# Gates multiplied into the activation, down results in two float32r parts, and the fallback block moved to expert 25

## The chip, the cores and the metric

The program runs on one core of a Trainium2 chip. The metric is the device time of one execution in microseconds, the median of three timed executions. The engines are TensorE (PE, which runs matrix products and, beside them, loads of the stationary operand, PEld), VectorE (DVE), ScalarE (ACT), GpSimd (POOL) and SyncE (SP, which issues most DMAs). In rows the suffix q (PEq, SPq) means the sequencer of the engine. Tokens are 256, in two halves of 128 called tt.

## The reference

One layer: a token mixer (two kinds of attention), a layer norm, a mixture of experts with four of 32 experts for each token, and a second layer norm. The change touches the experts alone:

```python
logits = xt @ w_router + b_router
top_val, top_idx = lax.top_k(logits, 4)
gates = softmax(top_val)
...
h = xblk @ w_up[e] + b_up[e]
gate = min(h[..., ::2], 7.0)
up = clip(h[..., 1::2], -7.0, 7.0)
act = (up + 1.0) * (gate * sigmoid(1.702 * gate))
yblk = act @ w_down[e] + b_down[e]
...
y = zeros.at[token].add(yblk * gate_of_token)
```

Everything is float32. `w_up[e]` is 1024 x 2048 (8 MB), `w_down[e]` 1024 x 1024 (4 MB), so 384 MB of expert weights are read once.

## The kernel before, in words

The mixer fills the first 241 us of the execution; it is the same in both kernels. Then one unrolled Python loop goes over the 32 experts. An expert has S = 64 slots. Tokens get into slots by one-hot products, not by indexed transfers, as follows.

- **Place and gather** (L696, L709). DVE compares a token's rank within the expert (`rankp`) with an iota and makes a bf16 one-hot `ph` (tokens x slots). 48 bf16 products (L714; 8 blocks of columns, 2 halves of tokens, 3 bf16 parts `hs` of the float32 activations) give `xg`, the 64 tokens of the expert, exact. The gather of expert e+1 runs inside expert e.
- **Up** (L731). A bias product (L741) starts each of two PSUM tiles h0 and h1; then 64 float32 products (L745) with the weights u0 and u1, 4 MB each. Each tile takes its half of the hidden columns.
- **SwiGLU** (L748) on DVE and ACT, into act0 and act1; **transposes** of both (L762, PSUM tile pt) and copies to actT (L763).
- **Down** (L765). 32 float32 products with the 4 MB d into PSUM (pd), copied to one of the two 64-row halves of `yb` (L928), which holds a pair of experts: an even one and the odd one behind it.
- **Way back** (L703, L720, L793). POOL makes `pg`, the one-hot of the pair times the gate, in float32; in the odd expert PE transposes it (L723) into `pgt`. In the next even expert `combine` adds the pair into the result `y` by four products that PE runs as float32 (eight rows of the trace, L796, 512 columns each). `y` stays in PSUM from the mixer to the end.

Each product of the combine and of the ups and downs is float32. `add_b_down` (L684) adds the down bias of all experts by the matrix of gates `gmat`; it is called in expert 22.

**Blocks that are rarely taken.** Tokens beyond 64 of an expert are handled by a first block at L896, behind the swiglu, and a second at L932, behind the down products. Each stands inside an If on a bit of a register; when it is not taken, every engine jumps over its code. In this input they are taken for experts 1 and 8. More than 128 tokens would need `general()` (L828), a loop over all experts whose code is emitted once, behind the last expert, inside an If at L969 that also holds a second copy of the final norm; it isn't taken here.

**Weights.** Five slots of 4 MB form a ring. Load k brings piece k of the order u0, u1, d of expert 0, 1, ... SP issues load(3e+5) and load(3e+6) behind the block at L896, and load(3e+7) at the end of expert e, behind the block at L932. Each load waits for PE to have read its slot.

**The order on PE** is the order of the code: bias, ups, (jump at L896), add_b_down in expert 22, combine in even experts, gather of the next expert, transposes, down, (jump at L932). There is no planner and no priority; what is written first goes first on each engine. At the end the last expert's down is cut in two halves (L777) with the combine of the first half in between, and `second_norm` (L946) writes the output.

Of the kernel before, what the change touches and what calls it, by code (L numbers as in the profile page):

```python
# [31 lines left out]
def tile_hybrid(ctx, tc, x, w_in, w_o, lambda_qk, subln_g, sinks, ln_g, ln_b,  # L32
                w_router, b_router, w_up, b_up, w_down, b_down, out):
    nc = tc.nc
# [36 lines left out]
    sel = keep.tile([96, NE], BF, name="sel")  # L71

# [343 lines left out]
    for k in range(3):  # L416
        nc.gpsimd.tensor_copy(sel[32 * k:32 * k + 32, :], ident[32 * k:32 * k + 32, 32 * k:32 * k + 32])
    for k in range(4):
        nc.gpsimd.tensor_copy(fold[32 * k:32 * k + 32, :], ident[32 * k:32 * k + 32, 32 * k:32 * k + 32])
# [230 lines left out]
    def gates():  # L650
        gate = mp.tile([128, 2, 4], F32, name="gate")
        gs = mp.tile([128, 2], F32, name="gs")
        eq = mp.tile([128, 2, 4, NE], F32, name="eq", tag="sg")
# [9 lines left out]
        nc.vector.tensor_reduce(gmat, eq.rearrange("p t k e -> p t e k"), AX.X, OP.add)  # L663

    def counts():
        cnt = mp.tile([1, 3, NE], F32, name="cnt", tag="sg")
# [17 lines left out]
    def add_b_down(bd):  # L684
# [3 lines left out]
        gT = mp.tile([NE, 2, 128], F32, name="gT", tag="sg")  # L688
# [14 lines left out]
    def place_back(pg, e, rk, r, n):  # L703

        for tt in range(2):
            nc.gpsimd.tensor_scalar(pg[:, tt], iota_s[:, None, :n].to_broadcast([128, r, n]), rk[:, tt:tt + 1],  # L706
                                    gmat[:, tt, e:e + 1], op0=OP.is_equal, op1=OP.mult)
# [11 lines left out]

    def way_back(pg, pgt=None, p=None):  # L720
# [3 lines left out]
        pgt = mp.tile([128, 2, 128], F32, name="pgt", tag="pgt") if pgt is None else pgt  # L724
# [23 lines left out]
    def swiglu(h, act, tmp=None):  # L748
        gt = h[:, :, :, 0].rearrange("p i c -> p c i")
        ut = h[:, :, :, 1].rearrange("p i c -> p c i")  # L750
        g, sg, u = tmp or (mp.tile([128, 2, 128], F32, name="g", bufs=1), mp.tile([128, 2, 128], F32, name="sg"),
# [5 lines left out]
        nc.vector.tensor_mul(act, u, sg)  # L757
# [7 lines left out]
    def down(d, n, actT, p=None):  # L765
# [4 lines left out]
        for k in range(8):  # L770
            q, c = divmod(k, 8 // G)
            for o in range(G):
                nc.tensor.matmul(p[o * n:(o + 1) * n, :w], actT[c // 2][:, c % 2, q * n:(q + 1) * n], d[:, k, o * w:(o + 1) * w],  # L773
                                 start=(k == 0), stop=(k == 7), tile_position=(0, o * n))
        return p

    def last_down(d, actT, yb):  # L777

        for ch in range(2):
            p = [pm.tile([128, 512], F32, name="pd", tag="m"), pm.tile([128, 512], F32, name="pd", tag=f"h{ch}", bufs=1)]  # L780
            for k in range(8):
                q, c = divmod(k, 4)
                for o in range(2):
                    cs = slice(ch * 512 + o * 256, ch * 512 + (o + 1) * 256)
                    nc.tensor.matmul(p[o][o * S:(o + 1) * S, :256], actT[c // 2][:, c % 2, q * S:(q + 1) * S], d[:, k, cs],
                                     start=(k == 0), stop=(k == 7), tile_position=(0, o * S))
# [35 lines left out]
    bd = mp.tile([NE, D], F32, name="bd", bufs=1)  # L822
    nc.sync.dma_start(out=bd, in_=b_down[0])
    xg_of, pgt, yb, pg = {}, None, None, None
    xg_of[0] = gather(place(rankp[:, :, 0], S), S)
    counts()
    gates()
    def general():  # L828

        d = ring[2]  # L830
# [4 lines left out]
        pgt2 = mp.tile([128, 2, 128], F32, name="pgt2", tag="pgt")  # L835
        pg2 = mp.tile([128, 2, 4, Q], F32, name="pg2", tag="pg")
# [3 lines left out]
        tmp = [mp.tile([128, 2, 128], F32, name=k, **kw) for k, kw in (("g", {"bufs": 1}), ("sg", {}), ("u", {"bufs": 1}))]  # L840
        m = [pm.tile([128, 512], F32, name=f"m{k}", tag="m") for k in range(2)]
        three = [m[k].rearrange("p (a b) -> p a b", b=128)[:, 0:2] for k in range(2)]
        for e in range(NE):
            def again(i):
                nc.sync.dma_start(out=df, in_=_rows(w_up, 128, e * D * 2048 + i * 8192, 16384, 8192))
                return d.rearrange("p (j a) c -> p j (a c)", a=2)

            with is_over(e, 1 if e else 0):
# [3 lines left out]
                with tc.For_i(1 if e else 0, n, 1):  # L852
                    nc.vector.tensor_scalar(rk, rk, float(Q), None, op0=OP.subtract)
                    place_back(pg2, e, rk, 4, Q)
                    place(rk, Q, ph2)
                    gather(ph2, Q, m[0].rearrange("p (a b) -> p a b", b=Q)[:, 0:8], xg2)
                    h2 = m[1].rearrange("p (i a b) -> p i a b", a=2, b=2)
                    for i in range(2):
                        up(e, Q, 0, h2, xg2, again(i), range(4 * i, 4 * i + 4))
                    swiglu(h2, act2, tmp)  # L860
                    nc.sync.dma_start(out=df, in_=_rows(w_down, 128, e * D * D, 8192, 8192))
                    more_down(d, act2, actT2, pg2, pgt2, yb2, three + [m[0]])
                    more_back(pgt2, yb2)

    for e in range(NE):
# [17 lines left out]
        if par == 1:  # L883
            pgt = way_back(pg)
        if e < NE - 2:
            for b in range(2):
                up(e, S, b, h[b], xg_of[e], u1, range(4, 8))
                swiglu(h[b], act[b])
        else:
# [3 lines left out]
            for b in range(2):  # L893
                swiglu(h[b], act[b])
        if e > 0:
            with is_over(e):  # L896
                act2 = mp.tile([128, 2, 128], F32, name="more", bufs=1)
                pg2 = mp.tile([128, 2, 4, Q], F32, name="pg2", tag="pg")
                rk = mp.tile([128, 2], F32, name="rk")
                nc.vector.tensor_scalar(rk, rankp[:, :, e], float(S), None, op0=OP.subtract)  # L900
                xg2 = gather(place(rk, Q), Q, pm.tile([128, 8, Q], F32, name="p", tag="h0", bufs=1))
                place_back(pg2, e, rk, 4, Q)
                h2 = h_tile(1)
                for i, u in enumerate((u0, u1)):
                    up(e, Q, 0, h2, xg2, u, range(4 * i, 4 * i + 4))
                swiglu(h2, act2)
# [7 lines left out]
        if e == 22:  # L914
# [7 lines left out]
        if par == 0:  # L922
            yb = mp.tile([128, 2, 512], F32, name="yb", bufs=1)
# [73 lines left out]
```

## Time and profile before

| | |
|---|---|
| timed executions | 1233.15, 1227.6, 1233.84 us (median 1233.15) |
| profiled execution, own time | 1228.62 us |
| its span in the profile | 1226.8 us |
| PE busy | 1105.1 us (90%) |
| DVE, ACT, POOL busy | 327.7, 200.8, 139.1 us |
| PEld (loads of stationary operands) busy | 514.3 us |
| DMA | 441.77 MB, mean 360 GB/s |

The page gives the busy time of each engine and 40 slices of the span, each about 30.7 us long. A digit is the busy share in tenths. In rows of a timeline the columns are the start in us from the start of the span, the length in us, the engine, the line of the kernel, the operation, the output and inputs, the tile's rows and columns, the type, and a count of joined instructions; in brackets stands the idle time of the engine before it and what ended that. "issue" in a bracket is time in which the engine waited for nothing that the profile shows. A line of the waits gives total idle time, how many times, and the longest.

### The profile page before, as it was taken

Reading aid. Unit: us, or ns where it says so; the run is one execution under the profiler, and the core shown is the slowest. Engines: PE = TensorE matmul, PEld = TensorE weight load, DVE = VectorE, ACT = ScalarE, POOL = GpSimd, SP = SyncE. Lnnn points to the kernel's source line nnn. Section 1 sums busy time; section 2 is a strip of 40 time slices with the busy share of each in tenths; the row PEclk is TensorE's granted clock in tenths of the full one; section 3 lists DMA queues with packets and bytes.
Section 4 is the critical chain, followed back from the end, with each engine's and each line's share of the span. In section 5 each row is a group of like instructions: output and inputs, shape, how many; then the busy total and the mean of one; then the engine's idle time right before and its main releaser. Section 6 shows DMA issues by size and latency. Waiting matters only on the chain. (4 is left out here: it accounts for less than half of the span.)

```text
span 1226.8 us, 17445 instructions
## 1 busy us (share of the span) xinstructions
PE 1105.1 (90%) x6841; PEld 514.3 (42%) x6841; DVE 327.7 (27%) x705; ACT 200.8 (16%) x425; POOL 139.1 (11%) x163
## 2 busy tenths in 40 slices
PE   7999999798989999989997999799998899979993
PEld 7989676333333333333332333233433233323332
DVE  4555964612111211221211111111121111111113
ACT  3765661401000000010000000000000000000000
POOL 1056562201000000000000000000000000000001
PEclk9999999899999999999998999899998899989998
DMA  9932528696799999969999999999999999999971
GB/s 327 360 131 119 206 82 330 248 418 271 292 426 423 420 426 426 427 276 427 427 426 425 426 426 426 427 426 426 425 425 426 402 408 422 425 427 418 420 298 39
DMA packets 46605, 441.77 MB, mean 360 GB/s; under 512 B 5120, under 2 KB 8320, under 8 KB 20512
## 3 DMA queue, kind: packets, MB, share of 16 engines
q1 hardware_dynamic: 46320, 439.52, 86.5%
q8 instruction: 101, 1.65, 0.5%
q14 instruction: 40, 0.33, 0.1%
q10 hardware_dynamic: 144, 0.26, 0.1%
HBM read 438.72 MB, written 1.05 MB: 358 GB/s over the span
## 5 line engine op out<-in xcount | busy, mean ns | idle before, releaser
L745 PE MATMUL h<-w,xg 128*64 128x512 f32 (+1 forms) x2176 | 470.2, 596 | 0.2 <-ACT xg L717 0.2
L745 PEld LDWEIGHTS h<-w,xg 128*64 128x64 f32 (+1 forms) x2176 | 150.2, 136 | 276.8 <-issue 265.4
L773 PE MATMUL pd<-w,actT 128*64 128x512 f32 x992 | 230.5, 616 | 0.3 <-issue 0.3
L773 PEld LDWEIGHTS pd<-w,actT 128*64 128x64 f32 x992 | 70.6, 142 | 138.9 <-issue 138.6
L706 POOL TENSOR_SCALAR pg<-iota_s,rankp,gmat 128x64 f32<-128x64 f32 x64 | 36.4, 581 | 792.9 <-PE p L723 773.5
L753 DVE TENSOR_SCALAR g<-h 128x256 f32<-128x256 f32 x66 | 28.0, 425 | 288.8 <-issue 159.1
L754 ACT ACTIVATE sg<-g 128x256 f32<-128x256 f32 x66 | 27.5, 417 | 468.9 <-DVE g L753 468.9
L714 PE MATMUL p<-ph,hs 128*128 128x64 bf16 (+1 forms) x1632 | 57.7, 197 | 37.5 <-issue 22.6
L161 POOL TENSOR_TENSOR lo<-w,hi 128x1024 fp32r<-128x1024 f32 x31 | 78.8, 2551 | 104.9 <-ACT hi L160 104.7
L928 DVE COPY yb<-pd 64x512 f32<-64x512 f32 x31 | 21.2, 684 | 247.3 <-PE pd L773 247.3
L714 PEld LDWEIGHTS <-hs 128*128 128x128 bf16 x1632 | 54.8, 101 | 62.0 <-issue 34.2
L796 PE MATMUL y<-yb,pgt 128*128 128x512 f32 x128 | 62.1, 628 | 8.4 <-DVE g L753 6.6
L928 ACT COPY yb<-pd 64x512 f32<-64x512 f32 x31 | 18.0, 582 | 238.9 <-DVE yb L928 135.7
L160 ACT CAST hi<-w 128x1024 fp32r<-128x1024 f32 x48 | 50.1, 1044 | 20.6 <-PE pj L199 13.8
L763 ACT COPY actT<-pt 128x256 f32<-128x256 f32 x64 | 23.9, 373 | 157.5 <-PE pt L762 157.2
L717 DVE COPY xg<-p 128x512 f32<-128x512 f32 x31 | 21.4, 691 | 100.7 <-PE p L714 100.7
L762 PE MATMUL pt<-ident,act 128*128 128x128 f32 x128 | 29.5, 316 | 19.2 <-ACT actT L763 16.8
L796 PEld LDWEIGHTS y<-yb,pgt 128*128 128x128 f32 x128 | 23.9, 197 | 47.1 <-issue 25.3
L188 PE MATMUL pj<-xh,hi 128*128 128x256 f32 x272 | 41.0, 295 | 2.3 <-ACT hi L160 1.6
L741 PE MATMUL h<-bups,sel 96*64 96x512 bf16 (+1 forms) x136 | 27.6, 420 | 16.0 <-PEq L932 16.0
L725 DVE COPY pgt<-p 128x256 f32<-128x256 f32 x18 | 7.6, 425 | 117.4 <-PE p L723 117.4
L188 PE MATMUL pj<-xl,hi 128*128 128x256 f32 x272 | 39.0, 287 | 0.0
(217 smaller groups left out, 825.2 us busy)
## 6 DMA issues: line engine op xcount, KB each, us to landing
w<-in_w_up_dram SPq DMA_DIRECT2D x120, 2048.0 KB, 22.1
w<-in_w_down_dram SPq DMA_DIRECT2D x58, 2048.0 KB, 15.0
w<-in_w_in_dram SPq DMA_DIRECT2D x5, 4096.0 KB, 16.4
w<-in_w_up_dram SPq DMA_DIRECT2D x16, 1024.0 KB, 18.8
w<-in_w_down_dram SPq DMA_DIRECT2D x12, 1024.0 KB, 13.1
w<-in_w_o_dram SPq DMA_DIRECT2D x2, 2048.0 KB, 11.1
w<-in_w_in_dram SPq DMA_DIRECT2D x1, 2048.0 KB, 15.1
w<-in_w_in_dram SPq DMA_DIRECT2D x1, 1536.0 KB, 10.7
```

What stands on the lines that cost most here:

```text
L160: nc.scalar.copy(hi, src)
L161: by.tensor_sub(lo, src, hi)
L188: nc.tensor.matmul(p[:, :256], a[:, j, :], b[:, j, :], start=(j == 0 and n == 0), stop=(j == 7 and n == 2))
L706: nc.gpsimd.tensor_scalar(pg[:, tt], iota_s[:, None, :n].to_broadcast([128, r, n]), rk[:, tt:tt + 1], gmat[:, tt, e:e + 1], op0=OP.is_equa ...
L714: nc.tensor.matmul(p[:, j, :], hs[:, tt, k, j, :], ph[:, tt, :], start=(tt == 0 and k == 0), stop=(tt == 1 and k == 2))
L741: nc.tensor.matmul(h[q * n:(q + 1) * n], sel[:, e:e + 1].to_broadcast([96, n]), cols16(bups, q), start=True, stop=False, tile_position=(0, ...
L745: nc.tensor.matmul(h[q * n:(q + 1) * n], xg[:, j, :], cols16(u[:, j % 4, :], q), start=False, stop=(j == 7), tile_position=(0, q * n))
L753: nc.vector.tensor_scalar(g, gt, 7.0, None, op0=OP.min)
L762: nc.tensor.transpose(p[:, c, :], act[:, c, :], ident)
L773: nc.tensor.matmul(p[o * n:(o + 1) * n, :w], actT[c // 2][:, c % 2, q * n:(q + 1) * n], d[:, k, o * w:(o + 1) * w], start=(k == 0), stop=( ...
L796: nc.tensor.matmul(y[tt][o], pgt[:, tt, :], yb[:, o, :], start=False, stop=last, skip_group_check=True)
L928: (nc.vector.tensor_copy, nc.scalar.copy)[o](yb[mine, o, :], p[o * S:(o + 1) * S, :])
```

## The change

Nothing of the mixer moves. In the experts:

- **Gates.** `gates()` also cuts `gmat` into three bf16 parts, `gm3`. For each expert a new `slot_gates` runs four bf16 products with 3 columns (L729 of the new kernel) that give each of the 64 slots its gate; the fifth operation of SwiGLU multiplies by it, so that act is already weighted. The gate is out of the way back.
- **Way back.** POOL's `place_back` and its pairs `pg` are gone from the main path. `turn_ranks` turns the ranks of all experts once; in each odd expert `ways_back` spreads two rows of them by four bf16 products (256 columns), and one DVE comparison with the slot's number gives the 0/1 matrix `wb`, in float32r, for the pair.
- **Down results** are kept as two float32r parts, `yh` (ACT's rounded copy) and `yl` (DVE's difference). The combine runs eight float32r products (L845) where it ran four float32 ones. The odd expert of a pair keeps its two column halves in the other order (swap), so that one product of 128 rows takes a part of each expert.
- **Bias.** `add_b_down` moves from expert 22 to expert 31, behind its ups and before its transposes. Its table is loaded with the last norm's tables into the freed slot.
- **PSUM.** The first transpose pair of an expert goes into bank h0 instead of the rotating m bank, and the slot gates share it.
- **Code.** `general()` is emitted at the end of expert 25 instead of behind the last one, with its loads in ACT's queue. The If at the end and the second copy of the norm are gone.

```diff
@@ def gates() @@
-        eq = mp.tile([128, 2, 4, NE], F32, name="eq", tag="sg")
+        eq = mp.tile([128, 2, 4, NE], F32, name="eq", tag="sg", bufs=1)
...
+        left = eq[:, :, 0]
+        for k in range(3):
+            nc.vector.tensor_copy(gm3[:, :, :, k], left if k else gmat)
+            if k < 2:
+                nc.vector.tensor_sub(left, left if k else gmat, gm3[:, :, :, k])
+
+    def turn_ranks():
+
+        p = pm.tile([128, 2, 128], F32, name="pr", tag="m")
+        for tt in range(2):
+            nc.tensor.transpose(p[:NE, tt, :], rankp[:, tt, :], ident)
+        nc.vector.tensor_scalar(rankT, p[:NE], NOT_HERE, None, op0=OP.add)
...
+    def slot_gates(ph, e, n, p, gs=None):
+
+        for tt in range(2):
+            for o in range(128 // n):
+                nc.tensor.matmul(p[o * n:(o + 1) * n], ph[:, tt, :], gm3[:, tt, e, :],
+                                 start=(tt == 0), stop=(tt == 1), tile_position=(0, o * n))
+        gs = mp.tile([128, 1], F32, name="gs") if gs is None else gs
+        nc.vector.tensor_reduce(gs, p, AX.X, OP.add)
+        return gs
...
+    halves = [slice(r * S, (r + 1) * S) for r in range(2)]
+
+    def ways_back(e):
+
+
+        p = pm.tile([128, 2, 256], F32, name="p2", tag="m")
+        for k in range(2):
+            for r in range(2):
+                one = e - 1 + (k if e == NE - 1 else r ^ k)
+                nc.tensor.matmul(p[halves[r], k, :], sel[:NE, one:one + 1].to_broadcast([NE, S]),
+                                 rankT.rearrange("p a b -> p (a b)"), start=True, stop=True, tile_position=(0, r * S))
+        wb = mp.tile([128, 2, 2, 128], F32R, name="wb", bufs=1)
+        nc.vector.tensor_scalar(wb.rearrange("p k a b -> p k (a b)"), p, slot[:, 0:1], None, op0=OP.is_equal)
+        return wb
...
-    def swiglu(h, act, tmp=None):
+    def swiglu(h, act, gs, tmp=None):
...
-        nc.vector.tensor_mul(act, u, sg)
+        nc.vector.scalar_tensor_tensor(act, u, gs, sg, op0=OP.mult, op1=OP.mult)
...
+    def keep_two(r, o, cs, p):
+
+        at = (halves[r], o, cs)
+        nc.scalar.copy(yh[at], p)
+        nc.vector.tensor_sub(yl[at], p, yh[at])
...
                 if ch == 1 and k == 3:
-                    combine(pgt, yb, (0,))
+                    last_back(0)
             for o in range(2):
-                (nc.vector.tensor_copy, nc.scalar.copy)[o](yb[S:, ch, o * 256:(o + 1) * 256],
-                                                           p[o][o * S:(o + 1) * S, :256])
-
-    def combine(pgt, yb, chs=(0, 1), last=False):
-        for tt in range(2):
-            for o in chs:
-                nc.tensor.matmul(y[tt][o], pgt[:, tt, :], yb[:, o, :], start=False, stop=last,
-                                 skip_group_check=True)
+                keep_two(o, ch, slice(o * 256, (o + 1) * 256), p[o][halves[o], :256])
+        last_back(1)
+
+    def back(at, o, rows, k, **kw):
+
+        for part in (yh, yl):
+            for tt in range(2):
+                nc.tensor.matmul(y[tt][o], at[rows, k, tt, :], part[rows, o, :], start=False,
+                                 stop=False, skip_group_check=True, **kw)
+
+    def last_back(ch):
+        back(wb, ch, slice(0, 128), 1)
+
+    def combine(at):
+        for o in range(2):
+            back(at, o, slice(0, 128), o)
...
-    bd = mp.tile([NE, D], F32, name="bd", bufs=1)
-    nc.sync.dma_start(out=bd, in_=b_down[0])
...
+    ph = place(rankp[:, :, 0], S)
+    xg_of[0] = gather(ph, S)
     counts()
     gates()
+    turn_ranks()
+    gs_of[0] = slot_gates(ph, 0, S, pm.tile([128, 3], F32, name="ps", tag="m"))
...
-        if par == 0:
-            pg = mp.tile([128, 2, 2, S], F32, name="pg", tag="pg")
-        place_back(pg[:, :, par:par + 1], e, rankp[:, :, e], 1, S)
...
         if par == 1:
-            pgt = way_back(pg)
+            wb = ways_back(e)
...
+                bd = tail[:NE, 2, :]
+                nc.sync.dma_start(out=bd, in_=b_down[0])
+        if par == 0 and e > 0:
+            combine(wb)
+        if e == NE - 1:
+            for r in range(2):
+                back(wb, r, halves[r], 0, tile_position=(r * S, 0))
+            for part in (yh, yl):
+                for r in range(2):
+                    nc.gpsimd.memset(part[halves[r], :, (1 - r) * 256:(2 - r) * 256].bitcast(F32), 0.0)
             add_b_down(bd)
-        if par == 0 and e > 0:
-            combine(pgt, yb)
+        ptg = pm.tile([128, 512], F32, name="ptg", tag="h0", bufs=1)
         if e + 1 < NE:
             xg_of[e + 1] = gather(ph, S, copy=nc.vector.tensor_copy)
-        for b in range(2):
-            trans(act[b], actT[b])
+            gs_of[e + 1] = slot_gates(ph, e + 1, S, ptg[:, 256:259])
+        trans(act[0], actT[0], ptg[:, :256].rearrange("p (a b) -> p a b", b=128))
+        trans(act[1], actT[1])
...
+            p = down(d, S, actT, swap=par)
+            for r in range(2):
+                keep_two(r, r ^ par, slice(0, 512), p[halves[r]])
...
+        if e == LATE:
+            with tc.If(words[4] > 0, preferred_fallthrough_block=False):
+                general()
         load(3 * e + 7)
-    combine(pgt, yb, (1,), last=True)
...
     second_norm()
-    with tc.If(words[4] > 0, preferred_fallthrough_block=False):
-        general()
-        second_norm()
```

The first place is the first expert on PE, behind the gather `p`. `pr` are the turned ranks, `ps` the slot gates of expert 0. Of before, from the last gather product to the first up product:

```order
L714 LDWEIGHTS hs
L714 MATMUL p<-ph_2261,hs 128x64
L741 LDWEIGHTS sel
L741 MATMUL h_2359<-bups,sel 64x512
L741 LDWEIGHTS sel
L741 MATMUL h_2359<-bups,sel 64x512
L745 MATMUL h_2359<-w_89,xg 64x512 x2
```

And of the changed kernel:

```order
L740 MATMUL p<-ph_2267,hs 128x64
L678 MATMUL pr<-ident,rankp 32x128 x2
L729 LDWEIGHTS ph_2267
L729 MATMUL ps<-gm_2265,ph_2267 64x3
L729 LDWEIGHTS ph_2267
L729 MATMUL ps<-gm_2265,ph_2267 64x3
L729 LDWEIGHTS ph_2267
L729 MATMUL ps<-gm_2265,ph_2267 64x3
L729 LDWEIGHTS ph_2267
L729 MATMUL ps<-gm_2265,ph_2267 64x3
L782 LDWEIGHTS sel
L782 MATMUL h_2378<-bups,sel 64x512
```

The bias products of expert 0 (h) stand behind the transposes of the ranks and the four slot gate products; `gm` is made by the gates.

The second place is PE behind the first rare block of an even expert (2), where the combine of experts 0 and 1 stands. Before:

```order
L896 UNCONDITIONAL_BRANCH
L796 MATMUL y_2054<-yb,pgt 128x512
L796 MATMUL y_2055<-yb,pgt 128x512
L796 MATMUL y_2056<-yb,pgt 128x512
L796 MATMUL y_2057<-yb,pgt 128x512
L714 LDWEIGHTS hs
L714 MATMUL p<-ph_2887,hs 128x64
```

Changed:

```order
L957 UNCONDITIONAL_BRANCH
L845 MATMUL y_2058<-yh,wb 128x512
L845 MATMUL y_2060<-yh,wb 128x512
L845 MATMUL y_2058<-yl,wb 128x512
L845 MATMUL y_2060<-yl,wb 128x512
L845 MATMUL y_2059<-yh,wb 128x512
L845 MATMUL y_2061<-yh,wb 128x512
L845 MATMUL y_2059<-yl,wb 128x512
L845 MATMUL y_2061<-yl,wb 128x512
L740 LDWEIGHTS hs
L740 MATMUL p<-ph_2928,hs 128x64
```

The combine's four float32 products became eight float32r ones, and the gather behind them did not move.

The third place is PE around `general()` (the loop that begins at L848 in the one and at L909 in the other). Before, behind the last expert's last combine:

```order
L932 UNCONDITIONAL_BRANCH
L796 MATMUL y_2055<-yb,pgt 128x512
L796 MATMUL y_2057<-yb,pgt 128x512
L969 COMPARE_AND_BRANCH
L969 UNCONDITIONAL_BRANCH
L848 REGISTER_ALU
```

Changed, behind the second rare block of expert 25, whose last product is the first row:

```order
L867 MATMUL y_2061<-yb_11723,pgt_11724 128x512
L1002 UNCONDITIONAL_BRANCH
L1009 COMPARE_AND_BRANCH
L1009 UNCONDITIONAL_BRANCH
L909 REGISTER_ALU
L909 COMPARE_AND_BRANCH
```

The jump over general() stands between experts 25 and 26 instead of behind all products.

## Rows read from the trace of the kernel before

**Rows 1.** The page's head: span, and the DMA share in 40 slices

```profile
span 1226.8 us, 17445 instructions
...
DMA  9932528696799999969999999999999999999971
```

**Rows 2.** Waits, PE and weight loads, 330 to 1180 us: total, times, longest

```profile
PE p L714 <- issue: 22.6, 6, 5.3
...
PEld h L745 <- DMA w<-in_w_up_dram: 0.4, 2, 0.2
```

**Rows 3.** Waits of SP, the queue of weight loads, whole span

```profile
SPq L96 <- PEq L896: 382.1, 27, 17.9
```

**Rows 4.** Timeline of PE, experts 20 and 21: start, length, work

```profile
850.92 0.42 PE L741 MATMUL h<-bups,sel 96*64 96x512 bf16 x2 [0.55 <-PEq L932]
...
866.54 3.70 PE L796 MATMUL y<-yb,pgt 128*128 128x512 f32 x8 [0.64 <-DVE g L753]
...
880.42 0.42 PE L741 MATMUL h<-bups,sel 96*64 96x512 bf16 x2 [0.56 <-PEq L932]
...
887.88 0.44 PE L723 MATMUL p<-ident,pg 128*128 128x128 f32 x2
...
896.09 1.56 PE L714 MATMUL p<-ph,hs 128*128 128x64 bf16 x48 [0.76 <-DVE g L753]
...
898.42 0.44 PE L762 MATMUL pt<-ident,act 128*128 128x128 f32 x2 [0.52 <-ACT actT L763]
...
906.52 0.42 PE L741 MATMUL h<-bups,sel 96*64 96x512 bf16 x2 [0.65 <-PEq L932]
```

**Rows 5.** Timeline of PE, gathers cut in two: experts 13, 18, 27

```profile
656.53 1.03 PE L714 MATMUL p<-ph,hs 128*128 128x64 bf16 x30 [0.66 <-DVE g L753]
662.07 1.14 PE L714 MATMUL p<-ph,hs 128*128 128x64 bf16 x18 [4.51 <-issue]
...
674.46 0.42 PE L741 MATMUL h<-bups,sel 96*64 96x512 bf16 x2 [0.64 <-PEq L932]
...
814.21 0.58 PE L714 MATMUL p<-ph,hs 128*128 128x64 bf16 x14 [1.25 <-issue]
...
1083.31 2.08 PE L714 MATMUL p<-ph,hs 128*128 128x64 bf16 x36 [4.93 <-issue]
```

**Rows 6.** Stretches: bounds, length, busy, PEclk, DMA share, GB/s

```profile
662.00:669.00 7.00, 6.41 (x34) 2.82 (x36) 0.69 (x1) 0.74 (x2) 0.00 (x0) 0.52 1.00 424
...
510.00:570.00 60.00, 54.29 (x379) 21.15 (x379) 9.92 (x24) 5.01 (x12) 2.27 (x4) 1.00 0.84 350
...
1180.00:1190.00 10.00, 9.43 (x46) 2.91 (x44) 1.11 (x2) 0.58 (x1) 0.00 (x0) 1.00 0.85 318
```

**Rows 7.** The page's DMA queues, code's queue: packets, MB, share

```profile
q8 instruction: 101, 1.65, 0.5%
```

**Rows 8.** Timeline of PE in the mixer: float32r products of 512 columns

```profile
129.79 1.19 PE L199 MATMUL pj<-hi,xh 128*128 128x512 f32 x4
...
132.73 1.08 PE L330 MATMUL sc<-sbT,vb 128*64 128x256 f32 x8
```

**Rows 9.** Timeline: first expert on PE, gates on DVE; expert 22

```profile
241.16 0.64 PE L741 MATMUL h<-bups,sel 96*64 96x512 bf16 x2
...
244.52 0.63 DVE L663 TENSOR_REDUCE gmat<-eq 128x64 f32<-128x256 f32 x1
...
923.58 6.12 PE L692 MATMUL y<-bd,gT 32*128 32x512 f32 x8 [1.61 <-DVE gT L689]
...
946.14 0.42 PE L741 MATMUL h<-bups,sel 96*64 96x512 bf16 x2 [0.56 <-PEq L932]
```

**Rows 10.** Timeline: last ups, last down products, last issue of outputs

```profile
1194.77 1.46 PE L745 MATMUL h<-w,xg 128*64 128x512 f32 x6
...
1199.36 5.40 PE L785 MATMUL pd<-w,actT 128*64 128x256 f32 x48
...
1214.31 3.68 SPq L965 DMA_DIRECT2D out_dram<-w  x3
```

More of the change, by code (lines that the diff above doesn't have):

```diff
@@ L71, in tile_hybrid @@
     sel = keep.tile([96, NE], BF, name="sel")
+    slot = keep.tile([128, 2], F32, name="slot")
+    nc.gpsimd.iota(slot, pattern=[[0, 2]], base=0, channel_multiplier=1, allow_small_or_imprecise_dtypes=True)
     def rstd_of(dst, var):
@@ L763, in trans, with down @@
         nc.scalar.copy(actT, p)
-    def down(d, n, actT, p=None):
+    def down(d, n, actT, p=None, swap=0):
         G = 128 // n
@@ L771, in down, with last_down @@
             q, c = divmod(k, 8 // G)
-            for o in range(G):
-                nc.tensor.matmul(p[o * n:(o + 1) * n, :w], actT[c // 2][:, c % 2, q * n:(q + 1) * n], d[:, k, o * w:(o + 1) * w],
-                                 start=(k == 0), stop=(k == 7), tile_position=(0, o * n))
-        return p
-    def last_down(d, actT, yb):
+            for r in range(G):
+                o = r ^ swap
+                nc.tensor.matmul(p[r * n:(r + 1) * n, :w], actT[c // 2][:, c % 2, q * n:(q + 1) * n], d[:, k, o * w:(o + 1) * w],
+                                 start=(k == 0), stop=(k == 7), tile_position=(0, r * n))
+        return p
+    def keep_two(r, o, cs, p):
+        at = (halves[r], o, cs)
+        nc.scalar.copy(yh[at], p)
+        nc.vector.tensor_sub(yl[at], p, yh[at])
+    def last_down(d, actT):
         for ch in range(2):
@@ L821, in tile_hybrid @@
     pm = ctx.enter_context(tc.tile_pool(name="pm", bufs=2, side="left", space=PSUM, reuse_waits="tile"))
-    bd = mp.tile([NE, D], F32, name="bd", bufs=1)
-    nc.sync.dma_start(out=bd, in_=b_down[0])
-    xg_of, pgt, yb, pg = {}, None, None, None
-    xg_of[0] = gather(place(rankp[:, :, 0], S), S)
+    yh, yl = (mp.tile([128, 2, 512], F32R, name=k, bufs=1) for k in ("yh", "yl"))
+    gm3 = mp.tile([128, 2, NE, 3], BF, name="gm3", bufs=1)
+    rankT = mp.tile([NE, 2, 128], BF, name="rankT", bufs=1)
+    xg_of, gs_of = {}, {}
+    ph = place(rankp[:, :, 0], S)
+    xg_of[0] = gather(ph, S)
     counts()
     gates()
+    turn_ranks()
+    gs_of[0] = slot_gates(ph, 0, S, pm.tile([128, 3], F32, name="ps", tag="m"))
     def general():
-        d = ring[2]
+        d = ring[SLOT]
         df = d.rearrange("p j c -> p (j c)")
@@ L844, in again @@
             def again(i):
-                nc.sync.dma_start(out=df, in_=_rows(w_up, 128, e * D * 2048 + i * 8192, 16384, 8192))
+                nc.scalar.dma_start(out=df, in_=_rows(w_up, 128, e * D * 2048 + i * 8192, 16384, 8192))
                 return d.rearrange("p (j a) c -> p j (a c)", a=2)
@@ L859, in general @@
                         up(e, Q, 0, h2, xg2, again(i), range(4 * i, 4 * i + 4))
-                    swiglu(h2, act2, tmp)
-                    nc.sync.dma_start(out=df, in_=_rows(w_down, 128, e * D * D, 8192, 8192))
+                    swiglu(h2, act2, gs2, tmp)
+                    nc.scalar.dma_start(out=df, in_=_rows(w_down, 128, e * D * D, 8192, 8192))
                     more_down(d, act2, actT2, pg2, pgt2, yb2, three + [m[0]])
                     more_back(pgt2, yb2)
+    LATE = 25
+    SLOT = (3 * LATE + 2) % 5
     for e in range(NE):
@@ L887, in tile_hybrid @@
                 up(e, S, b, h[b], xg_of[e], u1, range(4, 8))
-                swiglu(h[b], act[b])
+                swiglu(h[b], act[b], gs_of[e])
         else:
@@ L893, in tile_hybrid @@
             for b in range(2):
-                swiglu(h[b], act[b])
+                swiglu(h[b], act[b], gs_of[e])
         if e > 0:
```

50 lines of the change are left out of this document (25 added, 25 removed).

## The prediction

> **What bounds the kernel now.** I read the page's head first, then the waits of PE and of SP over the stage of the experts, then the timeline of one undisturbed pair of experts, then the places where PE stands still, and last the stretch in which the loads end.
>
> The head shows DMA nearly full from the eleventh slice on [rows 1], which looks like a kernel bound by its weights. The waits say otherwise: between 330 and 1180 us the ups waited for a weight load 0.4 us in all, in 2 waits [rows 2], while SP, which issues the loads, stood for PE 382.1 us behind the block at L896 alone [rows 3]. Slots come free too late; PE is the bound. But the margin is thin. An undisturbed pair (experts 20 and 21) takes PE 906.52 - 850.92 = 55.6 us [rows 4]. Its weights are six pieces of 4.19 MB, 25.2 MB, which at 424 GB/s [rows 6] take 59.3 us. So PE is ahead of the loads in an undisturbed pair and loses its lead elsewhere. At the end the DMA share is 0.85 in 1180 to 1190 [rows 6], so the last load lands near 1188.5, while the last down products start at 1199.36 [rows 10]: some 11 us of slack. No saving on PE can be worth much more than that unless the loads get earlier as well.
>
> Where PE loses time that no data explains: six gathers are cut in the middle, 22.6 us in all, "issue" as the reason, the longest 5.3 [rows 2]. Three of the six stand in [rows 5]: 4.51 us in expert 13, 1.25 in 18, 4.93 in 27. The cut costs more than its own length. From the gather's start in expert 13 to the next expert's bias product it is 674.46 - 656.53 = 17.93 us [rows 5], in the undisturbed expert 21 it is 906.52 - 896.09 = 10.43 [rows 4]: 7.5 us for a stall of 4.51, because behind it the granted clock is 0.52 in 662 to 669 [rows 6], about the 1.2 GHz level. At that ratio (1.66) the six cost 37.6 us, say 38.
>
> What are they? The queue named instruction carries 101 packets, 1.65 MB [rows 7], that is 16.3 KB for each. All six stand shortly behind the skipped block at L896. I counted instruction places on PE in the listing (one for a load, a register operation or a plain product, two for a transpose, four for a float32 product). The products at which the six gathers resume then lie 28, 11, 3, 14 and 11 times 256 places apart, within one. So code arrives in pieces of 256 places, and a jump that enters a new piece near its end reaches the next piece before it has come. Expert 13 ran 30 gather products first and expert 27 12 [rows 5], and the later the cut, the shorter the wait: the next piece was there some 6 us after the jump in each.
>
> [...]
>
> **The change part by part.** The sum is against the profiled execution's own 1228.62 us, of which 1226.8 are its span [rows 1].
>
> *Combine.* Four float32 products, eight rows, take 3.70 us [rows 4]. Float32r products of the same 512 columns: twelve in 132.73 - 129.79 = 2.94, 0.245 each [rows 8]. Eight of them 1.96, so -1.74 each, 15 times: -26. Bounds: as slow as float32 rows (0.46 each, no gain) or half that.
>
> *First transpose pair into h0.* The second pair now waits 0.52 for ACT's copy of the first [rows 4], since the two share a rotating bank. With another bank it need not. I take 0.36 of the 0.52, since the second act is late too: 31 times, -11. Bounds 0 and -16.
>
> *Slot gates.* Four bf16 products with a load each. A gather product with its load is 1.56 / 48 = 0.033 us [rows 4], so four are 0.13, 31 times: +4. Bounds 0 and +26, by a bias product (0.42 / 2 = 0.21 [rows 4]); that has 512 columns and the gather's 64, these have 3, so I take the gather's.
>
> *Ways back.* Two float32 transposes, 0.44 us [rows 4], against four bf16 products of 256 columns; the bias product, bf16 of 512 columns, is 0.42 for two [rows 4], so four halves are 0.42. Nothing, taken as +1 over 16 pairs; bounds -3 and +5.
>
> *SwiGLU, copies, POOL.* The fifth operation has one more operand; `keep_two` makes ACT and DVE work one after the other, where both copied at once. DVE and ACT stand idle for most of an expert, and the combine comes 16 us behind the copies [rows 4], so this is hidden, except behind the last product: +0.7. POOL's work leaves the main path, where nobody waited for it.
>
> *Bias.* In expert 22 `add_b_down` ran 6.12 us behind a wait of 1.61 for gT [rows 9], and the expert took 946.14 - 906.52 = 39.6 us [rows 4, 9], against 29.5 for expert 20 [rows 4]: its removal is worth -10.1. In expert 31 the same eight rows, at the combine's 0.46 each 3.7, with transposes and a part of the wait for gT: +4.5, on the path, since the down products at 1199.36 [rows 10] stand behind them. Bounds +2 (the wait runs beside the activation) and +10.
>
> *Start.* Slot gates of expert 0 stand ahead of its ups. `gmat` is done at 244.52 + 0.63 = 245.15 [rows 9]; five small DVE operations of about 0.2 make gm3, so PE's bias products go from 241.16 [rows 9] to about 246.5: +5.4. PE stands still for that time, and I add 1.5 for a lower clock behind it: +7. Bounds +3 (the loads' slack takes a part later) and +9.
>
> *If at the end.* The last output is issued at 1214.31 + 3.68 = 1217.99 [rows 10] and the span ends at 1226.8: 8.8 us. About 2.7 are the transfer; of the remaining 6.1 I give 4.5 to the jump over general() and the code behind it: -4.5. Bounds 0 and -5.5.
>
> Without code that is -26 - 11 + 4 + 1 + 0.7 - 10.1 + 4.5 + 7 - 4.5 = -34.
>
> *Code.* Counting places in the same way in the changed kernel, I look for jumps at L957 that enter a new piece with fewer than 110 places left to its end (beyond that the down products, four places each, keep PE busy until the piece is there). Odd experts: 5 (12 left), 7 (70), 15 (46), 23 (24), 25 (82), 29 (32), and 17 (106). Even ones, where the combine takes 16 places and 2 us first: 6 (53), 14 (29), 16 (88), 22 (7), 24 (65), 28 (15), 30 (72). Fourteen, against six before. The block grew from 234 places to 251, so nearly every jump now enters a new piece. The six odd ones cost as the long ones before (4.5 to 5.3 us times 1.66), 8.1 each, 48.5; expert 17 4.2; seven even ones 4.0 each (a stall of about 2.4), 28. And the jump over general(), now between experts 25 and 26 with all of PE's queue behind it, lands some 13,700 places on and must fetch: +6. Together 86.5 against 38: +48. Bounds: 35 (the fourteen as expert 18's 1.25 [rows 5], 2.1 each, and the 6) and 120 (all at 8, and 8).
>
> Sum: -34 + 48 = +14, 1242.6 against the profiled execution's own 1228.62. The median of the runs lies 4.5 above that execution, but stalls shrink where the loads would bound, so I add nothing and say 1243.
>
> **The rivals.**
>
> *A: code costs no more than now.* If the layout's phase is other than I count, or the prefetch takes such jumps when fewer loads are outstanding, code stays at 38 and -34 is what PE gains. It can't have it all, since loads bound then. The last up piece lands one piece (9.9 us) ahead of 1188.5, at 1178.6; I let the last 1 us of its products follow, so the ups end at 1179.5 instead of 1194.77 + 1.46 = 1196.2 [rows 10]: -16.7. The dip of 510 to 570, where the share is 0.84 [rows 6], fills by up to 9.6 of that, the start takes 7 of it back: -2.6 more. With the tail's +4.5, +0.7 and -4.5 it is -18.6: 1210. For it: six stalls are a small number to fix a phase from. Against: five multiples of 256, within one, don't come by chance.
>
> *B: between.* About half of the new cost comes: +24 - 34 = -10 on PE; 1219 with all of it, 1235 where the loads' slack of 11 and the tail take some: the middle near 1229.
>
> *C, slower by more: every one of the fourteen costs as the long ones.* When PE has less work per pair, SP's loads come closer together, and code's packets wait behind more of them; fourteen times 8, plus 8 at general(): 120, 120 - 38 - 34 = +48, 1277. It decides from about nine long stalls on. Expert 18's 1.25 in an even expert [rows 5] speaks against it.
>
> *D: the products in float32r cost 0.46 each*, as float32 ones do for half the work (3.70 / 8 [rows 4]): +26 on mine: 1269. The mixer's products [rows 8] speak against it, though their columns were not behind a one-hot.
>
> **How the numbers follow.** The likeliest, code eats the saving, 1234 to 1262: 0.45. A 0.25, B 0.17, C 0.08, D 0.05. The likeliest's own range comes from the bounds of code (35 and 120 are far off; 75 to 105 are the fourteen with even ones at 2 to 6 us) and of the start. The range from A's 1210 to 1262 leaves out C, D and the lower part of A, some 2 in 10. Half a per cent is what the three executions can tell from none: 1227 to 1239.3. Slower: 0.35 of the likeliest's 0.45, C and D: 0.48. Faster: A and the lower half of B: 0.33. The same: the rest, 0.19.
>
> **What would show it.** Right: cuts with "issue" in the gathers of experts 5, 7, 15, 23, 25 and 29 of 4 to 5 us and in some even ones of 1 to 4, at products that lie multiples of 256 places apart, half clock behind them, a stop of about 6 us between experts 25 and 26; combine near 2 us; expert 0's ups near 246.5; under 2 us less than 6.1 from the last output to the end. Wrong: less than 40 us of code stalls in all, or ups that wait for weights in the hundreds of nanoseconds each expert, which would be A; a combine near 3.7, D.

## The result, and the profile after

The changed kernel took 1279.09 us (median of four executions, 1277.37 to 1281.07) against 1232.6 of the kernel before in the same comparison (four, 1227.6 to 1233.84): ratio 1.0386, interval 1.0352 to 1.0419. The forecast was 1243, the range 1210 to 1262. The direction was right and the time is outside the range, at the price of rival C (1277), but not for C's reason, as the experiments show. The profiled execution's span is 1275.6 us against 1226.8 [rows 1], 48.8 more.

The page of the changed kernel, its head and the queue that brings code:

```profile
span 1275.6 us, 17843 instructions
PE 1108.1 (87%) x7027; PEld 525.0 (41%) x7027; DVE 363.4 (28%) x780; ACT 217.4 (17%) x458; POOL 104.0 (8%) x104
...
DMA  9933436686699999759999999999999997999940
...
q8 instruction: 105, 1.72, 0.6%
```

PE was busy 1105.1 us before and 1108.1 now, with eight cheaper rows in each combine. So 46 us of the 49 are time in which PE stood still. That the busy time did not fall goes with the lower clock behind the stops: the mean granted clock is 0.945 of full speed, against 0.970 before. The waits of PE, 330 to 1240 us, in the order of [rows 2]:

```profile
PE p L740 <- issue: 39.9, 11, 5.7
PE ptg L803 <- DVE gs L732: 19.8, 29, 1.0
...
PE h L782 <- issue: 8.4, 1, 8.4
...
PE y L845 <- issue: 4.6, 1, 4.6
PE pd L815 <- ACT actT L804: 4.4, 18, 0.2
PE ptg L729 <- issue: 3.4, 1, 3.4
PE p L764 <- DVE yl L823: 2.5, 1, 2.5
```

Two things are to be seen. The waits for code ("issue") grew from 22.6 us to 39.9 + 8.4 + 4.6 + 3.4 = 56.3. And a wait stands here that no row of before has: the first transposes of an expert (ptg) wait for VectorE's sum of the slot gates, 0.68 us each, 29 times.

Experts 20 and 21, undisturbed. Of the kernel before, two rows of PE that belong between those of [rows 4], the gather of expert 20 and the down products of expert 21:

```profile
870.08 1.56 PE L714 MATMUL p<-ph,hs 128*128 128x64 bf16 x48
...
898.78 7.09 PE L773 MATMUL pd<-w,actT 128*64 128x512 f32 x32
```

Of the changed kernel, first PE, then VectorE between the gather and the transposes of expert 21:

```profile
896.43 0.73 PE L845 MATMUL y<-yh,wb 128*128 128x512 f32 x2 [0.66 <-PEq L957]
...
898.41 1.57 PE L740 MATMUL p<-ph,hs 128*128 128x64 bf16 x48
...
909.38 0.42 PE L782 MATMUL h<-bups,sel 96*64 96x512 bf16 x2 [0.56 <-PEq L1002]
...
925.02 1.56 PE L740 MATMUL p<-ph,hs 128*128 128x64 bf16 x48 [0.77 <-DVE g L794]
926.51 0.23 PE L729 MATMUL ptg<-gm,ph 128*64 128x3 bf16 x4
927.43 0.44 PE L803 MATMUL ptg<-ident,act 128*128 128x128 f32 x2 [0.69 <-DVE gs L732]
927.71 0.38 PE L803 MATMUL pt<-ident,act 128*128 128x128 f32 x2
928.33 7.09 PE L815 MATMUL pd<-w,actT 128*64 128x512 f32 x32 [0.24 <-ACT actT L804]
936.07 0.42 PE L782 MATMUL h<-bups,sel 96*64 96x512 bf16 x2 [0.65 <-PEq L1002]
```

```profile
926.62 0.69 DVE L743 COPY xg<-p 128x512 f32<-128x512 f32 x1 [0.51 <-PE p L740]
927.23 0.15 DVE L732 TENSOR_REDUCE gs<-ptg 128x1 f32<-128x3 f32 x1
```

The combine takes 898.41 - 896.43 = 1.98 us against 870.08 - 866.54 = 3.54 before (its end is the start of the gather; 866.54 is in [rows 4]): -1.56, the forecast said -1.74. But from the gather's start to the down products it is 928.33 - 925.02 = 3.31 us, against 898.78 - 896.09 = 2.69 before: +0.62 in each undisturbed expert, where the forecast had -0.36 + 0.13 = -0.23. The gate products are done at 926.74. Their sum on VectorE stands behind the copy of the gathered tokens (0.69 us). The first transposes stand behind the sum, since they write the PSUM tile that it reads (ptg), and the second ones, into another tile (pt), stand behind the first on PE. The odd expert is longer than before, 936.07 - 909.38 = 26.69 against 26.10.

The cut in expert 5's gather (12 places left by the count), and the stop behind the jump over general():

```profile
420.58 0.31 PE L740 MATMUL p<-ph,hs 128*128 128x64 bf16 x5 [0.66 <-DVE g L794]
426.62 2.48 PE L740 MATMUL p<-ph,hs 128*128 128x64 bf16 x43 [5.74 <-issue]
```

```profile
1057.86 8.68 PE L815 MATMUL pd<-w,actT 128*64 128x512 f32 x32 [0.24 <-ACT actT L804]
1074.96 0.64 PE L782 MATMUL h<-bups,sel 96*64 96x512 bf16 x2 [8.41 <-issue]
```

Five products and their loads are ten places, and then PE waits. Behind it the granted clock is 0.50. There a pair of rows of the down products, 512 columns each, starts 0.85 us before the next pair (432.01 and 432.86 us), and from 433.4 us on, at a clock of 1.00, 0.43 us. That is 1.2 and 2.4 columns a nanosecond, and all that the traces show of the level that the prediction calls 1.2 GHz. The stretch at 0.50 (bounds, length, busy times, clock, DMA share, GB/s):

```profile
427.00:433.00 6.00, 5.31 (x54) 3.50 (x53) 0.76 (x2) 0.74 (x2) 0.00 (x0) 0.50 1.01 426
```

Where the 48.8 us are, by the starts of the experts on PE in the two traces (an undisturbed even expert 28.8 before and 27.9 after, an odd one 25.95 and 26.65):

| place | before | after | difference |
|---|---|---|---|
| start of expert 0 | 241.16 | 243.31 | +2.2 |
| expert 0 | 24.5 | 27.4 | +2.9 |
| experts 1 and 8, rare blocks taken | 46.5 and 49.8 | 51.7 and 54.1 | +9.5 |
| expert 22 (bias out, -10.7; cut in, +7.0; work -0.9) | 39.6 | 34.95 | -4.7 |
| 27 others: undisturbed work | | | -1.9 |
| 27 others: above undisturbed (cuts, the stop) | 42.0 | 80.3 | +38.3 |
| expert 31 to the end of the span | 45.5 | 48.1 | +2.6 |

### The profile page after: what moved, and what is told of

The parts are those of the page before. It is cut to its first block, busy times and chain, and to the rows that moved or that the text cites. A ratio compares the mean times of both kernels' runs of the same rounds, so it can differ in the third digit from the quotient of the medians.

```text
span 1275.6 us, 17843 instructions
## 1 busy us (share of the span) xinstructions
PE 1108.1 (87%) x7027; PEld 525.0 (41%) x7027; DVE 363.4 (28%) x780; ACT 217.4 (17%) x458; POOL 104.0 (8%) x104
## 5 line engine op out<-in xcount | busy, mean ns | idle before, releaser
L815 PE MATMUL pd<-w,actT 128*64 128x512 f32 x992 | 238.9, 637 | 5.3 <-ACT actT L804 4.9
L823 DVE TENSOR_TENSOR yl<-pd,yh 64x512 fp32r<-64x512 f32 (+1 forms) x66 | 44.4, 673 | 327.0 <-ACT yh L822 308.9
L740 PE MATMUL p<-ph,hs 128*128 128x64 bf16 (+1 forms) x1632 | 62.1, 201 | 54.9 <-issue 39.9
L795 ACT ACTIVATE sg<-g 128x256 f32<-128x256 f32 x66 | 27.5, 417 | 472.3 <-DVE g L794 472.3
L822 ACT CAST yh<-pd 64x512 fp32r<-64x512 f32 (+1 forms) x66 | 37.4, 566 | 264.5 <-PE pd L815 231.9
L804 ACT COPY actT<-ptg 128x256 f32<-128x256 f32 x32 | 11.9, 372 | 172.4 <-PE ptg L803 172.4
L190 PE MATMUL pj<-xh,lo 128*128 128x256 f32 x272 | 38.1, 283 | 0.0
L190 PEld LDWEIGHTS pj<-xh,hi 128*128 128x128 f32 x272 | 35.8, 195 | 3.5 <-issue 1.0
L758 DVE TENSOR_SCALAR wb<-p,slot 128x512 fp32r<-128x512 f32 x16 | 12.0, 751 | 84.8 <-PE p L755 84.8
L190 PEld LDWEIGHTS pj<-xl,hi 128*128 128x128 f32 x272 | 35.8, 196 | 0.0
## 6 DMA issues: line engine op xcount, KB each, us to landing
w<-in_w_in_dram SPq DMA_DIRECT2D x1, 2048.0 KB, 14.6
```

Of the source, the lines that this page charges most:

```text
L190: nc.tensor.matmul(p[:, :256], a[:, j, :], b[:, j, :], start=(j == 0 and n == 0), stop=(j == 7 and n == 2))
L740: nc.tensor.matmul(p[:, j, :], hs[:, tt, k, j, :], ph[:, tt, :], start=(tt == 0 and k == 0), stop=(tt == 1 and k == 2))
L795: nc.scalar.activation(sg, g, AF.Sigmoid, scale=1.702)
L815: nc.tensor.matmul(p[r * n:(r + 1) * n, :w], actT[c // 2][:, c % 2, q * n:(q + 1) * n], d[:, k, o * w:(o + 1) * w], start=(k == 0), stop=( ...
L822: nc.scalar.copy(yh[at], p)
L823: nc.vector.tensor_sub(yl[at], p, yh[at])
```

## The experiments

Seven kernels ran beside the kernel before, which gave 1229.68 us (seven runs) beside experiments 1 to 4 and 1230.45 (thirteen) beside 5 to 7. Beside the changed kernel it gave 1232.6, so differences of two or three microseconds between groups are not to be read.

**1. No jump lands near the end of a piece.** In the changed kernel, transposes are added inside the block behind the down products, which experts 1 and 8 alone run (they get none), and inside general().

```diff
-        for tt in range(2):
+        for tt in [0] * pads + [0, 1]:
             nc.tensor.transpose(p[:, tt, :], pg[:, tt].rearrange("p o s -> p (o s)"), ident)
...
-                more_down(d, act2, actT2, pg2, pgt2, yb2)
+                more_down(d, act2, actT2, pg2, pgt2, yb2, pads=PADS.get(e, 0))
```

PADS is 8 or 9 in most even experts and 22 in most odd ones.

> The changed kernel with extra transposes inside the second skipped block (never run in these experts) and in general(), so that the jump behind the ups of every expert from 3 to 31 lands 194 to 195 places ahead of the next piece of 256. Theory (places): the cuts of the gathers, 11 of 40 us in the changed kernel with their half clock about 75 us in all, are gone; the stop behind the jump over general() (8.4 us) stays. PE gains 75, the loads then bound: 1205 to 1225 us. Rival (the cuts come from loads that crowd out code's packets, wherever a jump lands): cuts move to other gathers, the time stays within 15 us of 1279.

Measured 1245.03 us (1243.04 to 1246.45), ratio 1.012 (1.010 to 1.0139). The waits of PE, 330 to 1300 us:

```profile
PE h L786 <- DMA w<-in_w_up_dram: 21.5, 11, 4.0
PE ptg L803 <- DVE gs L732: 20.9, 29, 1.0
...
PE y L708 <- DMA w<-in_b_down_dram: 9.9, 1, 9.9
...
PE h L782 <- issue: 7.9, 1, 7.9
```

No gather is cut any more; the stop at general() is the one large "issue" left. Not one instruction that runs in these experts was added or taken away, only the addresses moved, and 34 us went. That it wasn't 54 or more has its reason in the same rows: PE now waits 21.5 us for weights (0.4 in [rows 2]) and 9.9 us for the bias table, whose load the change had put behind the last weights; the transposes' wait, 20.9 us, is untouched. The theory of places holds; the estimate of the time missed its range by 20 us. The loads come later here than in the kernel before: from 240 to 360 us they move 299 GB/s, there 351, and the last weights land at 1208.0 us, there at 1188.4.

**2. All jumps near the end of a piece.** The same kernel with other numbers (63 and 50 transposes in experts 3 and 4), so that by the count about 30 places are left in every expert from 5 on, expert 8 aside.

> The same padding, chosen so that the jump behind the ups lands about 30 places ahead of the next piece in every expert from 5 on. Theory (places): every gather from expert 5 on, 25 of them without expert 8, is cut, against 13 experts that lost time in the changed kernel, each at 4 to 8 us: 1279 + 11 x 4 to 11 x 7.5 = 1323 to 1362 us, cuts all after the same number of products. Rival (crowding by loads): no more cuts than now, since PE works the same: 1265 to 1290.

Measured 1308.32 us (1305.98 to 1311.08), ratio 1.0636 (1.0613 to 1.0659). Experts 12 and 13, cut after 6 products in the even expert and 15 in the odd one, as nearly all up to expert 25 are, and the waits:

```profile
677.93 0.35 PE L740 MATMUL p<-ph,hs 128*128 128x64 bf16 x6
679.48 1.39 PE L740 MATMUL p<-ph,hs 128*128 128x64 bf16 x42 [1.20 <-issue]
...
707.06 0.61 PE L740 MATMUL p<-ph,hs 128*128 128x64 bf16 x15 [0.55 <-DVE g L794]
710.41 1.14 PE L740 MATMUL p<-ph,hs 128*128 128x64 bf16 x33 [2.74 <-issue]
```

```profile
PE p L740 <- issue: 53.2, 23, 4.9
...
PE y L845 <- issue: 6.4, 4, 1.8
```

Of the 25 gathers 22 are cut in their products (the 23rd stop of the row is one of 0.23 us in expert 4), and in front of the other three, in experts 26, 28 and 30, PE stops in the combine. So where the jump lands decides whether there is a cut. Behind general() the count is not exact: the cuts of the changed kernel come some 14 places sooner than counted in experts 29 and 30, which fits the stops in the combine here.

The time is below the expected 1323. A stop is 53.2 / 23 = 2.3 us here against 39.9 / 11 = 3.6 in the changed kernel. A part of such a difference could come from where the cut lies, but the whole time from the gather's start to its resumption shows it too: 710.41 - 707.06 = 3.35 us in expert 13 here, 426.62 - 420.58 = 6.04 in expert 5 of the changed kernel. The trace has fewer loads under way: when the ups end, mostly one transfer of weights (2 MB) is issued and not landed here, and two to five in the changed kernel, where the two experts that have one (7 and 25) have their next piece as early as here. So many cuts made each one shorter, where C gave each of fourteen the price of the long ones. No run changed the loads alone.

**3. general() back at the end.**

```diff
-        if e == LATE:
-            with tc.If(words[4] > 0, preferred_fallthrough_block=False):
-                general()
...
     second_norm()
+    with tc.If(words[4] > 0, preferred_fallthrough_block=False):
+        general()
+        second_norm()
```

> The changed kernel with general() and its If back behind the last norm, as before. Theory (places): the stop of 8.4 us ahead of expert 26 is gone, and experts 28 to 31 lie elsewhere by 13,729 places, so that the jumps of 29 and 30 land 198 and 238 places ahead of a piece instead of 32 and 72: 8.0 + 5.9 + 8.4 + 1.5 gained, 4.6 given back at the end: 1260 us (1255 to 1265). Rival (the stop is the price of having PE wait for its register, and moves with the If): 1279 - 8.4 + 8 = about 1279.

Measured 1259.12 us (1257.47 to 1259.87), 20.0 below the changed kernel. The stop is gone, as are the cuts of experts 29 and 30, which take 26.69 and 27.99 us as undisturbed ones do. Expert 26 starts with the ordinary wait:

```profile
1065.71 0.42 PE L782 MATMUL h<-bups,sel 96*64 96x512 bf16 x2 [0.65 <-PEq L1002]
```

**4. Slot gates in another PSUM tile.**

```diff
-            gs_of[e + 1] = slot_gates(ph, e + 1, S, ptg[:, 256:259])
+            pgs = pm.tile([128, 512], F32, name="pgs", tag="h1", bufs=1)
+            gs_of[e + 1] = slot_gates(ph, e + 1, S, pgs[:, :3])
```

> The changed kernel with the four slot gate products in a PSUM tile of bank h1 instead of the tile of the first transposes; nothing else moves, no place of the code either. Theory: the wait of 0.69 us for VectorE's sum of the gates ahead of every first transpose (19.8 us in 29 waits) goes, and the down products start 0.58 earlier: 31 times, -18, 1261 us (1257 to 1266). Rival: the transposes wait for the activation or ScalarE's copies instead, -0 to -5: 1274 to 1279.

Measured 1259.81 us (1258.76 to 1261.47), 19.3 below the changed kernel. PE between the gather and the down products of expert 21, beside it VectorE's sum, which now comes after the transposes began:

```profile
911.08 1.56 PE L740 MATMUL p<-ph,hs 128*128 128x64 bf16 x48 [0.77 <-DVE g L794]
912.57 0.23 PE L729 MATMUL pgs<-gm,ph 128*64 128x3 bf16 x4
...
912.73 0.44 PE L803 MATMUL ptg<-ident,act 128*128 128x128 f32 x2
913.00 0.38 PE L803 MATMUL pt<-ident,act 128*128 128x128 f32 x2
...
913.28 0.15 DVE L732 TENSOR_REDUCE gs<-pgs 128x1 f32<-128x3 f32 x1
...
913.63 1.94 PE L815 MATMUL pd<-w,actT 128*64 128x512 f32 x8 [0.24 <-ACT actT L804]
```

913.63 - 911.08 = 2.55 us, against 3.31 in the changed kernel and 2.69 before. So the bank h0 for the first transposes and the four products together are worth -0.14, near the -0.23 of the forecast; what spoiled it is the gates in the same tile. 0.76 in 31 experts is 23.6 us; the cuts of the gathers grew from 39.9 to 44.0 and took 4 of it back. The gates moved to another tile and another bank at once, so which of the two the wait goes by is not shown.

**5. The sum ahead of the copy.** The gates stay where the change has them; `gather` calls `slot_gates` between its products and its copy.

```diff
-        copy(xg, p)
+        if between:
+            between()
+        copy(xg, p)
```

> The changed kernel, with VectorE's sum of the gates issued ahead of its copy of the gathered tokens; the slot gates stay in the tile of the first transposes. Theory (the transposes wait for the sum, and that stands behind a copy of 0.69 us): the wait goes from 0.69 to about 0.3, 31 times, -12: 1267 us (1262 to 1271). Rival (the tile's sharing itself costs, whatever stands ahead on VectorE): 1276 to 1281.

Measured 1274.64 us (1272.11 to 1275.87), 4.5 below the changed kernel: between the two expectations. By the ratios to the kernel before, 1.0351 (1.0309 to 1.0394) against 1.0386 (1.0352 to 1.0419), this gain is not clear of noise; that the wait shrank is clear in the trace. The wait fell as the theory said, from 19.8 to 7.7, and an undisturbed expert by 0.4 (27.5 and 26.2); but the cuts grew:

```profile
PE p L740 <- issue: 43.2, 11, 5.9
...
PE ptg L805 <- DVE gs L732: 7.7, 29, 0.4
```

With the clock behind them (an estimate, 3.3 us at 1.5 times their length, since in the changed kernel code took 87.3 us with stops of 56.3) the cuts gave some 5 us back, and experts 7 and 9 are 2.7 and 1.7 us longer than in the changed kernel. That this is all of the missing 7 us was not shown.

**6. The kernel before without its cuts.** The edit of the first experiment on the kernel before (PADS 22 and 33 in most experts, general() as it was).

> The kernel before, with extra transposes in the second skipped block alone, so that the jump behind the ups of experts 3 to 31 lands 199 to 201 places ahead of the next piece of 256. Theory (places): its six cuts (22.6 us, about 38 with their half clock) go, and PE waits for loads instead, which bound then: 1205 to 1218 us. Rival (before, the cuts were hidden, since the loads bound anyway): 1225 to 1234, as now.

Measured 1216.37 us (1215.41 to 1217.45), ratio 0.9884 (0.9845 to 0.9923). It beats both kernels. The waits of PE, 330 to 1215 us:

```profile
PE h L745 <- DMA w<-in_w_up_dram: 14.6, 6, 4.1
...
PE h L741 <- issue: 4.4, 1, 4.4
```

The one "issue" is a stop at the start of expert 8, told of below.

The cuts of before were worth 14 us of the 38 that I counted for them. The rest goes into the waits for weights, 14.6 us, and the new stop, behind which 60 rows of the ups take 15.45 us, 0.26 each, where 28 rows of expert 9 in the kernel before take 6.17, 0.22 each, at a clock of 1.00: the loads bound.

**7. All repairs together on the changed kernel**: experiments 1, 3 and 4, and the bias table loaded ahead of the last down weights.

```diff
+            if e == NE - 2:
+                bd = ring[3 * NE % 5][:NE, 2, :]
+                nc.sync.dma_start(out=bd, in_=b_down[0])
             load(3 * e + 5)
```

> The changed kernel with no cuts (194 to 195 places ahead), slot gates in bank h1, general() and its If at the end as before, and the bias table loaded ahead of the last down weights. Theory: PE alone would need 1279 - 75 - 18 - 4 - 10, below 1190; the loads bound, which start their rings later here than in the kernel before by 3 us in the first expert and 5 in each of the two rare blocks: 1212 to 1228 us, ups that wait for weights in most experts from 16 on. Rival (PE still the bound, each fix moves its time to another wait): 1235 or more.

Measured 1224.95 us (1221.49 to 1226.46, ten runs), ratio 0.996 (0.994 to 0.9979). PE waits for weights in 25 places:

```profile
PE h L786 <- DMA w<-in_w_up_dram: 37.5, 25, 4.2
```

The last weights land at 1190.45 us, and at 1189.61 in experiment 6: the loads set the time of both, and what the changed kernel saves on PE in between gains nothing here. What is left is the tail, from the last landing to the end of the span: 1221.1 - 1190.45 = 30.7 us against 1213.9 - 1189.6 = 24.3, where the changed kernel has the bias; that the bias is all of it was not tried.

## Why the prediction was wrong, point by point

**What bounds.** Right: PE before, with some 11 us of slack to the loads. Experiment 6 shows both halves: without cuts the kernel gains 14 us and waits for its weights.

**Code.** Right in place, and in the total, partly by luck. The forecast was 86.5 us for thirteen to fourteen places and general(); the experts named for it took 87.3 above the undisturbed: 5 (8.0), 6 (5.8), 7 (4.1), 14 (6.6), 15 (7.8), 16 (4.0), 17 (5.6), 22 (7.0), 23 (8.1), 24 (3.2), 25 with general() (11.5), 26 (1.6), 29 (8.0), 30 (6.0). The parts were off both ways and made up for each other: the six even ones took 32.6, where seven at 4.0 were forecast, the odd ones 5, 7, 15, 23 and 29 took 36.0 where I had 8.1 each, 25 and 26 with general() 13.1 where I had 14.1, and 17 took 5.6 where I had 4.2. Of the fourteen only expert 28 is whole. Code's packet came there about 3 us before the jump; why is not shown, since the count behind general() is some 14 places off. Experiments 1 and 2 show by moving addresses alone that the places decide.

One reading of the prediction was too simple. Where the jump lands PE ran on at once, five products in expert 5, and waited 5.74 us where the next piece begins; so the cuts are waits for the piece behind the jump's target. The wait for the target itself is the stop behind general(), which I had put at 6 us by estimate: 8.41 us before the first product, and gone in experiment 3. Where code ran straight on, the next piece was there in time, and this is what the runs show of what the prediction calls the prefetch: in experiment 1 the ups waited for "issue" 0.7 us in all, in 2 waits.

**The step that failed** is "First transpose pair into h0 ... I take 0.36 of the 0.52 ... 31 times, -11", with "Slot gates ... +4". I priced the four products on PE and the bank, and not the wait that comes with sharing it. Measured +0.62 in each expert, some +19, where these two said -7: 26 us of the 36 by which the forecast missed. The rare blocks are 9.5 more, for which the sum had no term. Experiment 4 shows the cause: with the gates in another tile, -19.3. The order printed ahead of the prediction has the four gate products in front of the transposes, and the text of the change says that they share the bank; who reads that bank, and what stands ahead of the reader on VectorE, I did not ask.

**Combine.** Right: 1.98 us for eight rows, -1.56 against -1.74, some -23 in all. Rival D (float32r at 0.46 each) is out. It was not undone by itself.

**Rare blocks.** The forecast had nothing for them: +9.5. In expert 8's second block the transposes of the way back wait 2.46 us where they waited 1.14: by the trace they start when VectorE has made yl from the tile pd (ScalarE's rounded copy, then the difference, for one half after the other). Behind the longer wait the 64 products take 5.18 us instead of 3.66, at a granted clock of 0.69 instead of 1.00:

```profile
545.46 0.44 PE L803 MATMUL pt<-ident,more 128*128 128x128 f32 x2
548.36 0.41 PE L764 MATMUL p<-ident,pg 128*128 128x128 f32 x2 [2.46 <-DVE yl L823]
549.38 5.18 PE L815 MATMUL pd<-w,moreT 128*32 128x256 f32 x64 [0.61 <-DVE pgt L766]
```

So "this is hidden" of `keep_two` was wrong where the rare block comes right behind the down products. The first block grew by about 2.4 as well. This was read from the trace and not tried; with the gates first (experiment 5) the same wait of 2.5 us is put down to POOL.

**Bias, start, end.** Bias in expert 22: -10.7 (forecast -10.1). In expert 31 the down products end 7.2 us later after its start (forecast +4.5): the eight rows of the bias take 4.46 us behind a wait of 1.56 for gT, the granted clock is 0.67 from 1248.0 to 1250.5 us, their second half, and the first 48 down products behind them take 7.40 instead of 5.40. Start and expert 0: +5.1 (forecast +7), but in other parts: the ups start at 243.31, 2.2 later and not 5.4, and expert 0 itself is 2.9 longer, with a granted clock of 0.79 over its first 13 us against 0.97. End: -4.6 from the last down product to the end of the span (forecast -4.5 + 0.7).

**The rivals.** The time is C's, 1277, by another way: code cost 87 and not 120, and the rest of the sum is some 37 us worse than -34, by the transposes' wait (26), the rare blocks (9.5) and small parts. C's price was a right number for a wrong reason. A (code costs no more than now) is out by the cuts. The chance of 0.13 for all above 1262 (C 0.08 and D 0.05) was too small: I let the sum's bounds count for the code alone, and none for a wait that the change adds.

**By the sum:** +48 for code became 87.3 - 42.0 = +45.3, and -34 for all the rest became 48.8 - 45.3 = +3.5.

## What to carry to other kernels

A product that is moved into a shared PSUM tile brings the tile's readers with it, here a wait of 0.68 us in 29 experts: ask who reads the tile, what stands ahead of that reader in its queue, and what writes the tile next, before pricing the product. In a long unrolled kernel with skipped blocks, count where the jumps land: here padding inside code that never runs was worth 34 us of the changed kernel and 14 of the one before. And a saving on the engine that bounds was worth only the lead of the next one, here about 14 us.

## What was not expected of the hardware

Cuts got shorter when more of them came: 2.3 us each in experiment 2 against 3.6, with fewer loads under way at each jump; the link is read from the traces and was not tried by itself.

A jump behind the down products stopped PE as well, in one place each of experiments 2 and 6, where the padding makes the block that it skips longer than 256 places. By the count it was 282 places behind expert 3 in experiment 2, and PE stood 6.81 us before the next expert's first product. It was 268 behind expert 7 in experiment 6, with 16 places left to the next piece, and PE ran seven rows of expert 8 and then stood 4.37 us:

```profile
386.05 0.64 PE L782 MATMUL h<-bups,sel 96*64 96x512 bf16 x2 [6.81 <-issue]
```

```profile
479.90 0.59 PE L741 MATMUL h<-bups,sel 96*64 96x512 bf16 x1 [4.37 <-issue]
```

Blocks of 156 to 256 places in the same spot did not stop it (252 behind expert 2 in experiment 6, 256 behind expert 4 in experiment 2). The jump over general(), some 13,700 places, cost 8.4.
